# Small row loads ahead of the first weight, and masks, a turned row and two norms behind the third and fourth tile's products

## The chip, the cores and the metric

The kernel runs on one core of a Trainium2 chip. The metric is the device time of one execution in microseconds. A core has TensorE (PE in the profile, its weight loads PEld), VectorE (DVE), ScalarE (ACT), GpSimd (POOL) and SyncE (SP), which here only issues DMAs. Each engine works through its own instructions in order; semaphores tie them together.

## What is computed

One layer of a bidirectional hybrid encoder over 1024 tokens of width 1024, in float32: a norm, one input projection, gated linear attention in both directions beside a pooling mixer, a gated merge with an output projection, then a norm and a SwiGLU feed-forward layer, and a final norm. Only the first two lines of the layer matter for the change:

```python
h = rmsnorm(x, norm_mix[l])
proj = h @ w_in[l]
q, k, v, r, lr_f, lr_b, u, g_a, g_b = jnp.split(proj, split_points, axis=-1)
log_a_f = jax.nn.log_sigmoid((lr_f @ w_decay_up_fwd[l] + b_decay_fwd[l])) / GATE_NORMALIZER
```

The other vectors (`norm_ffn`, `gla_norm`, `pool_scale` and the two decay biases) and the causal masks are used only later in the layer.

## The kernel before

Tokens come in eight tiles of 128. Every float32 operand of a product is split into a high and a low part, and a product is three matmuls: high by high, high by low, low by high (line 275).

The opening computes the value columns of the first two heads, tile by tile. A tile `x` is loaded by `load_x`; its norm is a Square with a sum on ScalarE (line 321, in halves line 463 for the first tiles), an addition on VectorE and a power on GpSimd (lines 306 and 307), and a scaling on VectorE into `xn` (line 311). TensorE turns `xn` by 128x128 pieces into a bank `tr` of PSUM (line 328), and `gain_and_split` reads the bank twice: ScalarE writes the high part `hh` (line 336), VectorE the low part `hl` (line 340), both with the gain that stands in `cols`. The pairs of features `hh`, `hl` are the stationary operands; the moving ones are the eight pieces of a weight, loaded into `vraw` (line 388) and split into `wv` (lines 201 and 202, the difference on VectorE or GpSimd).

`pair_products` multiplies: first tiles 0 and 1 together, with the splitting of the weights and the norms of tiles 2 and 3 in between (`first_steps`), then tile 2, between whose first steps the features of tiles 2 and 3 are turned (`next_steps`), then tile 3. What comes out is split again into `vh` on ScalarE and `vl` on VectorE (lines 515 and 517). `low_rank` follows with `lw`, a split small weight (`lraw`), at line 561, and then the projections of the heads.

The order of the work around these products is set by hand. After every product `pump` advances a clock by one (by the width of the product over 512), and a generator that stands in `side` issues its next step when its delay has run down: `begin(norms(4), 1)` asks for the norm of tile 4 one product later, and `norms` then asks for two more until the norm of tile 5.

Small vectors are loaded as rows (line 374), `rows[0]` for the first gain and `rows[1]` for five others; `columns` turns such rows on TensorE (bank `vps`, line 454) and copies them into `cols` on VectorE (line 455). `masks` writes the masks `keep` and `carry` on VectorE (lines 131 to 133); both are used only in the attention.

All loads named here are issued on SP. A DMA bears one of eight semaphores in turn (DMAHW0 to DMAHW7), and a DMA waits until the earlier one that bears its semaphore has landed.

Of the kernel before, what the change touches and what calls it, by code (L numbers as in the profile page):

```python
# [54 lines left out]
def kernel(  # L55
# [38 lines left out]
    def name(s):  # L94
        count[0] += 1
        return f"{s}_{count[0]}"

    def slot(dtype=F32, shape=(2, HALF), s="slot"):
        return slots.tile([P, *shape], dtype, tag="slot", name=name(s))
# [10 lines left out]
    def bank(pool, s="ps"):  # L110
        return pool.tile([P, HALF], F32, tag=pool.name, name=name(s))

    def as_f32(ap):
        return ap.bitcast(F32)
# [14 lines left out]
    def masks():  # L129
        for n in range(4):  # L130
            nc.vector.tensor_copy(keep[:, n, :], keepf[:, :P])
        nc.vector.memset(carry[:, :, :], 1.0)
        nc.vector.memset(carry[:, :, 0:1], 0.0)
# [56 lines left out]
    def begin(gen, delay=0.0):  # L190
        side.append([gen, delay])

    def finish_side():
        while side:
            for _ in side[0][0]:
                pass
            side.pop(0)
# [49 lines left out]
    def fetch():  # L247
        src = next(order, None)
        if src is not None:
            loaded.append(load(*src))  # L250

    def prepare():
        if not loaded:
            fetch()
        if loaded:
            ready.append(Weights(loaded.pop(0)))

            credit[0] = -2.0
# [18 lines left out]
    def mm3(ps, a, b, first, last, onto=False):  # L277
        products(ps, a, b, first, last, onto)
        pump(ps.shape[-1] / HALF)
# [15 lines left out]
    def tokens(pair, t):  # L295
        return tuple(p[:, (t % 4) * P : (t % 4 + 1) * P] for p in pair)
# [53 lines left out]
    def to_features(xn, t0, act, gain):  # L350

        for kp in range(KT // 2):
            ps = bank(ps_g, "tr")
            for i in range(2):
                transpose_tile(ps, xn[i], i, kp)
            gain_and_split(ps, kp, t0, act, gain)
            yield 1
# [5 lines left out]
    rows = [tmp.tile([n, P], F32, tag="t2", name="rows") for n in (8, 32)]  # L363
# [9 lines left out]
    def load_rows(dst, at, v, n):  # L373
        nc.sync.dma_start(dst[at : at + n, :], v[0].rearrange("(j p) -> j p", p=P))
# [7 lines left out]
    def load_pair_weights(n):  # L382
        for _ in range(n):
            k = len(pair_raw)
            if k % 2 == 0:
                vraw.append(slot(s="vraw"))
            raw = vraw[-1][:, k % 2, :]
            nc.sync.dma_start(raw, w_in[k * P : (k + 1) * P, V0 : V0 + 2 * DV])
            pair_raw.append(raw)
# [7 lines left out]
    def load_other_rows(*which):  # L397
        for i in which:
            load_rows(rows[1], sum(n for _, n in vec_rows[1:i]), *vec_rows[i])
# [1 line left out]
    load_x(0, 2)  # L401
    load_x(1)
    load_rows(rows[0], 0, *vec_rows[0])
    load_other_rows(1, 2)
    load_pair_weights(6)
    load_x(2)
    load_pair_weights(1)
    load_x(3)
    load_pair_weights(1)
    nc.sync.dma_start(lraw[:, :, :], w_in[:, LR0:U0].rearrange("(k p) c -> p k c", p=P))  # L410
    load_other_rows(3, 4, 5)
    nc.gpsimd.memset(uraw[:, :, :, :], 0.0)

    hT = Activations("h")
# [1 line left out]
    def norm_x(t):  # L416
        rs = norm_scale(xt[t % 4][:, :], xn[t % 4], "n1")
        scale_by(xn[t % 4][:, :], xt[t % 4][:, :], rs)
        if t + 4 < NT:
            load_x(t + 4)  # L420

    def norms(t0):
        for t in (t0, t0 + 1):
            norm_x(t)
            yield 2
# [26 lines left out]
    def columns(src, at, n):  # L452
        vps = bank(ps_g, "vps")
        nc.tensor.transpose(vps[:, :n], src[:, :], ident[:n, :n])
        nc.vector.tensor_copy(cols[:, at : at + n], vps[:, :n])
# [45 lines left out]
    def pair_products(ts, before=None):  # L501
        banks = [bank(ps_mm) for _ in ts]
        for k in range(KT):
            if before:
                before(k)
            for ps, t in zip(banks, ts):
                mm3(ps[:, :], tokens(hT(k, t // 4), t), pair_w[k], k == 0, k == KT - 1)
        for ps, t in zip(banks, ts):
            for h in range(2):
                if t // 4 == len(pair_v[h]):  # L510
                    pair_v[h].append((slot(F32R, (4, DV), "vh"), slot(F32R, (4, DV), "vl")))
            parts = [[part[:, t % 4, :] for part in v[t // 4]] for v in pair_v]
            halves = [ps[:, h * DV : (h + 1) * DV] for h in range(2)]
            for (hi, _), src in zip(parts, halves):
                nc.scalar.copy(hi, src)
            for (hi, lo), src in zip(parts, halves):
                nc.vector.tensor_tensor(lo, src, as_f32(hi), op=ALU.subtract)
# [19 lines left out]

    next_features = to_features(xn[2:], 2, hT, g_mix)
    pair_products((0, 1), first_steps)
    masks()  # L540
    columns(rows[1], 8, 32)
    fetch()
    begin(norms(4), 1)
    for d, w_up in enumerate((w_decay_up_fwd, w_decay_up_bwd)):
        for i in range(4):
            load_up(i, d, w_up)
    pair_products((2,), next_steps)
    finish_side()
    begin(norms(6), 0.5)
    begin(to_features(xn, 4, hT, g_mix), 1)  # L550
    begin(to_features(xn[2:], 6, hT, g_mix), 2)
    low_rank_weights()
    prepare()
    pair_products((3,))
    lrT = slot(F32R, (2, HALF), "lrT")

    def low_rank(half):
# [1467 lines left out]
```

## Time and profile before

| | us |
|---|---|
| median of three runs | 1384.52 (1384.5 to 1385.35) |
| profiled execution | 1383.06 |
| its span | 1381.0 |
| TensorE busy | 1367.8 |
| VectorE, ScalarE, GpSimd busy | 835.4, 641.7, 748.6 |
| TensorE's waits for hl (line 340), two of them | 1.3 |

The mean granted clock of TensorE is 0.999 of full speed. Times in the rows of the trace are from the span's start. A row of the timeline has its start, its duration, engine, line, operation, what is written and read, and in brackets the idle time of that engine just before it with what ended it. Matmuls are pipelined, so that rows of TensorE overlap, and the distance of two starts tells its pace better than the durations.

### The profile page before, as it was taken

The page shows a single profiled execution, that of the slowest core. Times are in us where ns is not written, and L with a number is a line of the kernel's source. Part 1 is how long each engine was busy: PE and PEld are TensorE (multiplying, and loading weights), DVE is VectorE, ACT ScalarE, POOL GpSimd, SP SyncE. Part 2 cuts the span into 40 slices and gives each one's busy share as a digit, 9 for nine tenths or more (in the row PEclk, how much of TensorE's full clock was granted, in tenths as well). Part 3 has the DMA queues.
Part 4 walks back from the last instruction along what each step waited for, and adds up shares of the span by engine and source line. Part 5 has one row for each costly group of instructions (what it writes and reads, how often), then busy time and mean ns, then how long its engine had stood idle before and what let it go on. Part 6 is the DMA issues. An engine that isn't in the chain of part 4 may idle for free. (4 is left out here: it accounts for less than half of the span.)

```text
span 1381.0 us, 18211 instructions
## 1 busy us (share of the span) xinstructions
PE 1367.8 (99%) x6514; PEld 1145.9 (83%) x6514; DVE 835.4 (60%) x1025; ACT 641.7 (46%) x1170; POOL 748.6 (54%) x554
## 2 busy tenths in 40 slices
PE   8999999999999999999999999999999999999998
PEld 7888899988888888888888888888888888888886
DVE  5364656567845886687884855555655556343374
ACT  6465756654334544554346633333333334444352
POOL 3222616132288546668665276666666667455453
PEclk9999999999999999999999999999999999999999
DMA  7111414322478668996517355555444447985561
GB/s 226 31 55 53 138 50 134 107 63 77 137 210 292 200 217 265 358 406 227 189 61 244 115 175 175 176 175 175 160 141 140 146 139 264 386 305 186 169 213 76
DMA packets 166730, 243.60 MB, mean 176 GB/s; under 512 B 10952, under 2 KB 95984, under 8 KB 166640
## 3 DMA queue, kind: packets, MB, share of 16 engines
q1 hardware_dynamic: 166496, 242.18, 52.1%
q8 instruction: 51, 0.84, 0.2%
q14 instruction: 39, 0.32, 0.1%
q10 hardware_dynamic: 144, 0.26, 0.0%
HBM read 164.55 MB, written 77.86 MB: 176 GB/s over the span
## 5 line engine op out<-in xcount | busy, mean ns | idle before, releaser
L202 POOL TENSOR_TENSOR wl<-fs,wh 128x512 fp32r<-128x512 f32 x120 | 167.4, 1399 | 160.2 <-ACT wh L201 103.3
L275 PE MATMUL ps<-gh,wh 128*128 128x512 f32 x616 | 240.5, 390 | 0.0
L275 PE MATMUL ps<-gl,wh 128*128 128x512 f32 x616 | 239.8, 389 | 0.3 <-DVE gl L1594 0.3
L275 PE MATMUL ps<-gh,wl 128*128 128x512 f32 x616 | 239.7, 389 | 0.0
L202 POOL TENSOR_TENSOR wl<-fraw,wh 128x512 fp32r<-128x512 f32 x90 | 129.5, 1439 | 63.6 <-ACT wh L201 61.2
L275 PE MATMUL ps<-hh,wh 128*128 128x512 f32 x376 | 151.7, 403 | 0.0
L202 POOL TENSOR_TENSOR ol<-gor,oh 128x1024 fp32r<-128x1024 f32 (+1 forms) x42 | 101.6, 2423 | 85.7 <-ACT oh L201 71.3
L275 PE MATMUL ps<-hh,wl 128*128 128x512 f32 x376 | 146.7, 390 | 0.0
L275 PE MATMUL ps<-hl,wh 128*128 128x512 f32 x376 | 146.5, 390 | 0.0
L275 PEld LDWEIGHTS ps<-gl,wh 128*128 128x128 f32 x616 | 115.6, 188 | 24.6 <-DVE gl L1594 0.7
L275 PEld LDWEIGHTS ps<-gh,wh 128*128 128x128 f32 x616 | 115.7, 188 | 24.0 <-ACT hb L1613 0.2
L275 PEld LDWEIGHTS ps<-gh,wl 128*128 128x128 f32 x616 | 115.6, 188 | 23.9
L202 POOL TENSOR_TENSOR wl<-raw,wh 128x512 fp32r<-128x512 f32 x40 | 55.0, 1385 | 120.9 <-ACT wh L201 111.1
L275 PE MATMUL ps<-oh,oh 128*128 128x512 f32 x308 | 119.8, 389 | 0.0
L275 PE MATMUL ps<-ol,oh 128*128 128x512 f32 x308 | 119.8, 389 | 0.0
L275 PE MATMUL ps<-oh,ol 128*128 128x512 f32 x308 | 119.8, 389 | 0.0
L202 POOL TENSOR_TENSOR wl<-wraw,wh 128x512 fp32r<-128x512 f32 x56 | 92.3, 1678 | 42.6 <-ACT wh L201 42.5
L202 DVE TENSOR_TENSOR ol<-wor,oh 128x1024 fp32r<-128x1024 f32 (+1 forms) x42 | 63.0, 1511 | 68.2 <-ACT oh L201 55.7
L201 ACT CAST wh<-fs 128x512 fp32r<-128x512 f32 x120 | 73.7, 614 | 27.8 <-DVE fs L1013 26.5
L275 PEld LDWEIGHTS ps<-hh,wl 128*128 128x128 f32 x376 | 70.6, 188 | 15.0
L275 PEld LDWEIGHTS ps<-hl,wh 128*128 128x128 f32 x376 | 70.8, 188 | 13.0
L275 PEld LDWEIGHTS ps<-hh,wh 128*128 128x128 f32 x376 | 70.7, 188 | 12.9
(269 smaller groups left out, 3116.9 us busy)
## 6 DMA issues: line engine op xcount, KB each, us to landing
fraw<-in_w_ffn_in_dram SPq DMA_DIRECT2D x44, 512.0 KB, 6.6
gor<-g_out SPq DMA_DIRECT2D x35, 512.0 KB, 7.4
g_out<-s SPq DMA_DIRECT2D x44, 256.0 KB, 2.0
raw<-in_w_in_dram SPq DMA_DIRECT2D x40, 256.0 KB, 4.2
fraw<-in_w_in_dram SPq DMA_DIRECT2D x20, 512.0 KB, 6.7
wor<-t_out SPq DMA_DIRECT2D x20, 512.0 KB, 5.4
g_out<-g SPq DMA_DIRECT2D x33, 256.0 KB, 2.6
x<-in_x_dram SPq DMA_DIRECT2D x15, 512.0 KB, 3.7
```

The lines of the kernel that those rows point to most:

```text
L201: nc.scalar.copy(hi, src)
L202: eng.tensor_tensor(lo, src, as_f32(hi), op=ALU.subtract)
L275: nc.tensor.matmul(ps, a[i], b[j], start=first and n == 0, stop=last and n == 2, skip_group_check=onto)
```

## The change

The loads of the third to fifth of the other rows move ahead of the weights on SP. `masks` moves from behind the products of tiles 0 and 1 to behind those of tile 3, and the turning of `rows[1]` to behind those of tile 2. The norms of tiles 4 and 5 get a delay of 3.5 in place of 1.

```diff
     load_rows(rows[0], 0, *vec_rows[0])
-    load_other_rows(1, 2)
+    load_other_rows(1, 2, 3, 4, 5)
     load_pair_weights(6)
...
     nc.sync.dma_start(lraw[:, :, :], w_in[:, LR0:U0].rearrange("(k p) c -> p k c", p=P))
-    load_other_rows(3, 4, 5)
...
     pair_products((0, 1), first_steps)
-    masks()
-    columns(rows[1], 8, 32)
     fetch()
-    begin(norms(4), 1)
+    begin(norms(4), 3.5)
...
     pair_products((2,), next_steps)
     finish_side()
+    columns(rows[1], 8, 32)
...
     pair_products((3,))
+    masks()
```

On SP, at the start of the program, the loads from the gain of the attention's norm to the tile 2 of `x` (`x_122`) stood so before, with the semaphores for which each waits:

```order
L374 DMA rows<-in_gla_norm_dram 8x128
L388 DMA vraw_138<-in_w_in_dram 128x512 x2
L388 DMA vraw_141<-in_w_in_dram 128x512 [waits DMAHW0_49]
L388 DMA vraw_141<-in_w_in_dram 128x512 [waits DMAHW1_49]
L388 DMA vraw_144<-in_w_in_dram 128x512 [waits DMAHW2_49]
L388 DMA vraw_144<-in_w_in_dram 128x512 [waits DMAHW3_49]
L371 DMA x_122<-in_x_dram 128x1024 [waits DMAHW4_49]
```

The same place now:

```order
L374 DMA rows<-in_gla_norm_dram 8x128
L374 DMA rows<-in_pool_scale_dram 8x128
L374 DMA rows<-in_b_decay_fwd_dram 4x128
L374 DMA rows<-in_b_decay_bwd_dram 4x128 [waits DMAHW0_49]
L388 DMA vraw_141<-in_w_in_dram 128x512 [waits DMAHW1_49]
L388 DMA vraw_141<-in_w_in_dram 128x512 [waits DMAHW2_49]
L388 DMA vraw_144<-in_w_in_dram 128x512 [waits DMAHW3_49]
```

DMAHW2 is borne by the load of the second tile, the third DMA of the program. Four weights were issued before the wait for it, and now there is one.

On VectorE, behind the products of tiles 0 and 1 (`ps_229` is the sum of tile 1, `tr_386`, `tr_404` and `tr_416` are the turned pieces of tiles 2 and 3, `x_120` is tile 4), the rows were:

```order
L517 TENSOR_TENSOR vl_355<-ps_229,vh_354 128x256
L131 CAST keep<-keepf 128x128 x4
L132 MEMSET carry 128x512
L133 MEMSET carry 128x8
L455 COPY cols<-vps_370 128x32
L340 SCALAR_TENSOR_TENSOR hl_261<-tr_386,cols,hh_260 128x256 x2
L306 TENSOR_SCALAR n1rs_400<-n1ms_398 128x1
L311 TENSOR_SCALAR xn_124<-x_120,n1rs_400 128x1024
L340 SCALAR_TENSOR_TENSOR hl_285<-tr_404,cols,hh_284 128x256 x2
L340 SCALAR_TENSOR_TENSOR hl_316<-tr_416,cols,hh_315 128x256 x2
```

There they are now (the turned pieces are called `tr_377`, `tr_389` and `tr_401`):

```order
L516 TENSOR_TENSOR vl_355<-ps_229,vh_354 128x256
L340 SCALAR_TENSOR_TENSOR hl_261<-tr_377,cols,hh_260 128x256 x2
L340 SCALAR_TENSOR_TENSOR hl_285<-tr_389,cols,hh_284 128x256 x2
L340 SCALAR_TENSOR_TENSOR hl_316<-tr_401,cols,hh_315 128x256 x2
L306 TENSOR_SCALAR n1rs_418<-n1ms_416 128x1
L311 TENSOR_SCALAR xn_124<-x_120,n1rs_418 128x1024
```

The masks and the copy have left this place, and the three pairs of `hl` stand ahead of the norm of tile 4.

Behind the products of tile 3 (`ps_453`), the masks stand on VectorE now between `vl` and the features of the tiles from 4 on:

```order
L516 TENSOR_TENSOR vl_355<-ps_453,vh_354 128x256
L131 CAST keep<-keepf 128x128 x4
L132 MEMSET carry 128x512
L133 MEMSET carry 128x8
L340 SCALAR_TENSOR_TENSOR hl_580<-tr_574,cols,hh_579 128x256 x2
```

Before, the last row followed the first one here directly.

## The prediction, made before the changed kernel ran

> **What bounds the kernel now.** I read the page's totals first, then the waits of TensorE over the whole span, to see whether anything but TensorE's own work sets the end.
>
> ```profile
> span 1381.0 us, 18211 instructions
> PE 1367.8 (99%) x6514; PEld 1145.9 (83%) x6514; DVE 835.4 (60%) x1025; ACT 641.7 (46%) x1170; POOL 748.6 (54%) x554
> PE ps L275 <- DVE hl L340: 1.3, 2, 0.7
> PE tr L328 <- DVE xn L311: 1.2, 1, 1.2
> PE op L275 <- DVE p L202: 0.4, 2, 0.2
> ```
>
> TensorE is busy for 99% of the span, and each wait row (total us, times, longest) is small. Of these three the first two lie ahead of 30 us; every other later wait is at most as long as the third. The busy time by stretch (TensorE first) says the same of the middle: 1 us idle in 500, and 0.7 in 700.
>
> ```profile
> 100.00:600.00 500.00, 498.99 (x2618) 428.33 (x2618) 318.31 (x443) 261.91 (x535) 245.14 (x188) 1.00 0.52 170
> 600.00:1300.00 700.00, 699.31 (x3112) 577.78 (x3111) 420.78 (x424) 292.46 (x458) 439.76 (x282) 1.00 0.57 195
> ```
>
> So a microsecond won or lost early reaches the end: later no wait is long enough to swallow it. The change acts before 50 us, and I look for what TensorE waits for there. The timeline of the third tile's products (start, duration, engine, idle before):
>
> ```profile
> 25.60 0.71 PE L275 MATMUL ps<-wv,hh 128*128 128x512 f32 x2
> 26.99 0.50 PE L275 MATMUL ps<-wv,hl 128*128 128x512 f32 x1 [0.68 <-DVE hl L340]
> 27.33 0.63 PE L275 MATMUL ps<-wv,hh 128*128 128x512 f32 x2
> 29.25 0.50 PE L275 MATMUL ps<-wv,hl 128*128 128x512 f32 x1 [0.61 <-DVE hl L340]
> 29.58 0.62 PE L275 MATMUL ps<-wv,hh 128*128 128x512 f32 x2
> 32.32 0.62 PE L275 MATMUL ps<-wv,hh 128*128 128x512 f32 x2
> 33.00 0.62 PE L275 MATMUL ps<-wv,hh 128*128 128x512 f32 x2
> ```
>
> One step of the contraction (two hh, one hl product) takes 33.00 - 32.32 = 0.68 us undisturbed. From 25.60 to 29.58 three steps should take 2.04 and take 3.98: the two waits, 1.29 us as idle rows, cost 1.94 us of cadence.
>
> **What the change takes away.** Both waits are for hl, which VectorE writes late. Its rows, with what ScalarE and GpSimd do beside:
>
> ```profile
> 23.82 1.41 DVE L517 TENSOR_TENSOR vl<-ps,vh 128x256 fp32r<-128x256 f32 x4
> 23.93 0.89 ACT L336 ACTIVATE hh<-tr,cols 128x256 fp32r<-128x256 f32 x2
> 24.66 1.12 ACT L321 ACTIVATE xn<-x 128x1024 f32<-128x1024 f32 x1
> 25.15 0.62 DVE L131 CAST keep<-keepf 128x128 uint8<-128x128 f32 x4
> 25.82 0.48 DVE L132 MEMSET carry<- 128x512 bf16 x1
> 26.46 0.87 DVE L340 SCALAR_TENSOR_TENSOR hl<-tr,cols,hh 128x256 fp32r<-128x256 f32 x2
> 27.46 0.55 POOL L307 TENSOR_TENSOR n1rs<-n1rs,half_neg 128x1 f32<-128x1 f32 x1 [7.20 <-DVE n1rs L306]
> 28.05 0.75 DVE L311 TENSOR_SCALAR xn<-x,n1rs 128x1024 f32<-128x1024 f32 x1 [0.66 <-POOL n1rs L307]
> 28.72 1.65 DVE L340 SCALAR_TENSOR_TENSOR hl<-tr,cols,hh 128x256 fp32r<-128x256 f32 x4
> 31.09 0.75 DVE L311 TENSOR_SCALAR xn<-x,n1rs 128x1024 f32<-128x1024 f32 x1 [0.66 <-POOL n1rs L307]
> 35.73 0.60 PE L328 MATMUL tr<-ident,xn 128*128 128x128 f32 x4
> ```
>
> First wait: the masks and the copy of the turned row hold VectorE from 25.15 to 26.46, while hh is ready at 24.82. Second: the norm of tile 4 makes VectorE idle 0.66 for GpSimd and then scale for 0.75, ahead of the hl. In the changed order the three hl pairs follow the vl directly: with 0.87 each they run at about 25.2 to 26.0, 26.0 to 26.9 and 26.9 to 27.8. Without waits TensorE wants the first hl at 26.06 (25.60 plus two products), when its first half has been written for 0.4 us; the second pair's first half is ready near 26.5 against 27.4 wanted, the third's near 27.4 against 28.8. ScalarE's Square also goes behind the hh, so these come earlier, not later. I take the whole 1.94, and 1.29 as the least.
>
> What is late next? The two delayed norms: their chain (Square 1.1, GpSimd 0.55, scaling 0.75) then ends near 31.2, where it ends now at 31.84 (31.09 + 0.75), and TensorE turns that tile at 35.73, 1.94 earlier after the change: 2.6 us of room. The turned row is 0.24 of TensorE in either place, and its column copy precedes nothing that waits: nothing.
>
> **The masks' new place.** They stand behind the fourth tile's vl:
>
> ```profile
> 41.96 0.74 DVE L517 TENSOR_TENSOR vl<-ps,vh 128x256 fp32r<-128x256 f32 x2
> 42.62 0.86 DVE L340 SCALAR_TENSOR_TENSOR hl<-tr,cols,hh 128x256 fp32r<-128x256 f32 x2
> 44.04 0.88 DVE L340 SCALAR_TENSOR_TENSOR hl<-tr,cols,hh 128x256 fp32r<-128x256 f32 x2 [0.56 <-ACT hh L336]
> ```
>
> About 1.2 us of masks (0.62 + 0.48 and a small one) delay these hl, of which 0.56 goes into VectorE's idle time. The cover is that the products then running use the first four tiles' features, and that five banks take the turned tiles. I charge 0; without the cover 1.2.
>
> **The opening, the uncertain term.** Three more row loads now pass SP ahead of the weights, and at most eight DMAs are outstanding by the semaphores in the order. So what waits for the second tile's landing (SP's wait of 2.0 us below) is no longer the fifth weight, but the second. The first weight goes out about 1 us later, by three row issues of some 0.3; ScalarE, which casts it ahead of the first hh, has 1.74 us of idle time there: hidden.
>
> ```profile
> 2.92 0.29 SPq L374 DMA_DIRECT2D rows<-in_gla_norm_dram  x1
> SPq L388 <- DMA x<-in_x_dram: 2.0, 1, 2.0
> 7.07 0.63 ACT L463 ACTIVATE xn<-x 128x512 f32<-128x512 f32 x1 [2.28 <-DMA x<-in_x_dram]
> 10.11 0.47 ACT L336 ACTIVATE hh<-tr,cols 128x256 fp32r<-128x256 f32 x1 [1.74 <-PE tr L328]
> 10.49 0.61 ACT L201 CAST wv<-vraw 128x512 fp32r<-128x512 f32 x1
> 17.51 0.63 ACT L201 CAST wv<-vraw 128x512 fp32r<-128x512 f32 x1
> 20.30 0.75 DVE L311 TENSOR_SCALAR xn<-x,n1rs 128x1024 f32<-128x1024 f32 x1 [0.85 <-POOL n1rs L307]
> 21.52 0.60 PE L328 MATMUL tr<-ident,xn 128*128 128x128 f32 x4
> vraw<-in_w_in_dram SPq DMA_DIRECT2D x1, 256.0 KB, 6.9
> x<-in_x_dram SPq DMA_DIRECT2D x2, 256.0 KB, 2.6
> GB/s 0 0 0 0 0 0 0 147 197 262 352 369 377 410 246 197 229 295 295 338 289 270 357 320 393 393 418 393 393 418 401 303 238 205 205 320 344 336 361 352
> DMA packets 2227, 3.21 MB, mean 321 GB/s; under 512 B 1182, under 2 KB 1198, under 8 KB 2227
> ```
>
> The 40 slices of the GB/s row are 0.25 us each from 0, the last row is the mean from 8 to 18 us; the 6.9 us to landing is the last weight's, issued at 9.33, so landed at 16.2.
>
> A gain: the second tile lands at 7.07, and the opening chain (its sum, the scalings, the turns, the first product) starts there. Summing the slices, 1.05 MB, the first two tiles, had moved by 5.45, and 1.64 MB by 7.0: weights moved beside the tile. With all but one weight out of its way it lands between 6.05 (5.45 plus 0.6, as the first half tile: moved by 2.8, landed at 0.80 + 2.6 = 3.4) and 7.07. I take the middle, 6.55: 0.5 us gained, bounds 0 and 1.02.
>
> A loss: the second weight goes out only then, so the DMA engines run dry. Now the fifth weight is issued at 7.07, and its bytes show about 1.6 us later, in the slices behind the 205s. From the second weight to the eighth with two tiles between there are 2.88 MB, 9.0 us at 321 GB/s. So the last weight lands at 6.55 + 1.6 + 9.0 + 0.6 and a little for a full queue, about 18.0. Wanted: from its cast at 17.51 to the fourth tile's scaling (20.30 + 0.75) are 3.54 us, and TensorE turns that tile at 21.52; so a landing after 17.98, less the 0.5 won, delays TensorE. That is 0.5 lost. The second weight lands near 6.55 + 2.6 = 9.2 to 10 and is cast at 10.49 now, about 10.0 then: in time. Gain and loss cancel: 0, with bounds of -1.0 and, if the second weight goes out at 7.07 and takes 4.75 us (the middle of 2.6 and 6.9), +1.3, its lateness against 10.49.
>
> Here a rule weighs in. The Trainium skill, DMA: Bandwidth & Descriptors, Queues, rings and completion order, says that an SDMA engine consumes the descriptors of a ring in order. By it weights issued behind the tile take nothing from it; the sum would be -1.4 instead of -1.9. The trace speaks half against it, by the 1.64 MB moved at a landing of a tile that stands within the first 1.05.
>
> **Sum.** -1.94 + 0 + 0 = -1.9 us. The profiled execution took 1383.06 (span 1381.0 and 2.06 around it), so 1381.1 by its own time; the runs' median, 1384.52, lies 1.46 above it, and the same step from there gives 1382.6.
>
> **The rivals.** (1) The tile lands no earlier, at 7.07, and the weights still lose 0.5: -1.94 + 0.5 = -1.4, 1383.1. For it: the ring's order; against it: the slices. (2) The tile lands at 6.05 and the stream keeps up: -1.94 - 1.02 = -2.96, 1381.6. For it: 400 GB/s slices; against it: the dry spell. (3) Masks in the new place delay TensorE by their 1.2: -0.7, 1383.8, if the half-filled VectorE there has less room than its idle row shows. (4) Slower: the load stream, restarted late, runs at the 205 GB/s of its weakest slices. 2.88 MB then take 14.0 us, the last weight lands at 7.07 + 1.6 + 14.0 + 0.6 = 23.3, 5.3 us late, and +3.4 is left: 1387.9. It turns the sign from a landing past 19.9 on; the mean of 321 speaks against it. That nothing changes is hardly possible: VectorE's order does change.
>
> **The numbers.** Forecast 0.46, rival 1 0.20, rival 2 0.22, rival 3 0.05, rival 4 0.07. 0.2% is 2.8 us, about what a measurement of this kernel can tell from no change; only rival 2 passes it downward and only rival 4 upward. So faster 0.22, same 0.71, slower 0.07. The range runs from just under rival 2, 1381.3, to the forecast with the least gain (1.29) and the most loss (1.3), 1384.5, rounded up.
>
> **Right or wrong.** The profile after should have no row of TensorE waiting for hl in the third tile's products, the two norms' Squares behind the hh, and the masks behind the fourth tile's vl with no new wait of TensorE. The second tile's landing, the second weight's cast and the fourth tile's turn give the opening: first hh 0.5 earlier, near 9.6, and the first turn of the third and fourth tiles near 21.5. I am wrong if TensorE waits for a wv or xn for over a microsecond before 22 us, or if a wait after 50 us takes the gain back.

## The result, and the profile after

The changed kernel takes 1380.62 us in the median (1380.12 to 1382.23, fourteen runs), and the kernel before, run in turn with it, 1383.77 (1382.81 to 1385.65, fourteen runs). The ratio is 0.9978, with a 95% interval from 0.9969 to 0.9986: a gain of 3.15 us, and of 1.9 to 4.3 by the interval. The forecast was 1382.6, its range began at 1381.3, and the result lies below it.

The profiled execution of the changed kernel took 1382.23 us, the most of its fourteen. Its totals, and the five longest waits of TensorE (total us, times, longest):

```profile
span 1380.2 us, 18211 instructions
PE 1368.3 (99%) x6514; PEld 1146.9 (83%) x6514; DVE 836.3 (61%) x1025; ACT 641.7 (46%) x1170; POOL 748.0 (54%) x554
PE warm L473 <- POOL ident masks.py:199: 1.4, 1, 1.4
PE vps L453 <- DMA rows<-in_norm_mix_dram: 1.2, 1, 1.2
PE sc L858 <- DVE st L842: 0.5, 2, 0.2
PE op L275 <- DVE p L202: 0.4, 2, 0.2
PE tr L328 <- DVE xn L311: 0.4, 1, 0.4
```

The row of 1.3 us for hl is gone. The middle is as idle as it was, 1.1 us in 500 and 0.7 in 700 (busy time by stretch, TensorE first), so no later wait took the gain back:

```profile
100.00:600.00 500.00, 498.89 (x2617) 428.05 (x2617) 318.26 (x442) 260.98 (x533) 243.89 (x187) 1.00 0.52 170
600.00:1300.00 700.00, 699.35 (x3112) 577.92 (x3111) 421.41 (x425) 292.45 (x459) 439.69 (x282) 1.00 0.57 195
```

The third tile's products in the timeline of the changed kernel, with the features, the norm and the turned row beside them:

```profile
24.42 0.19 PEld L275 LDWEIGHTS ps<-wv,hl 128*128 128x128 f32 x1 [0.28 <-DVE hl L340]
24.68 1.41 DVE L516 TENSOR_TENSOR vl<-ps,vh 128x256 fp32r<-128x256 f32 x4
24.78 2.58 ACT L336 ACTIVATE hh<-tr,cols 128x256 fp32r<-128x256 f32 x6
26.00 2.44 DVE L340 SCALAR_TENSOR_TENSOR hl<-tr,cols,hh 128x256 fp32r<-128x256 f32 x6
26.24 0.71 PE L275 MATMUL ps<-wv,hh 128*128 128x512 f32 x2
27.02 0.62 PE L275 MATMUL ps<-wv,hh 128*128 128x512 f32 x2
27.71 0.62 PE L275 MATMUL ps<-wv,hh 128*128 128x512 f32 x2
28.39 0.62 PE L275 MATMUL ps<-wv,hh 128*128 128x512 f32 x2
29.25 0.75 DVE L311 TENSOR_SCALAR xn<-x,n1rs 128x1024 f32<-128x1024 f32 x1 [0.66 <-POOL n1rs L307]
30.52 0.24 PE L453 MATMUL vps<-ident,rows 32*128 32x32 f32 x1
```

The six hl follow each other in one row of 2.44 us, and three steps take 28.39 - 26.24 = 2.15 us where they took 3.98: 1.83 won. A smaller wait ahead of them is new: with the turned row gone from its old place, TensorE comes sooner to the product of an earlier hl, and loading that hl as weights waits 0.28 (the row at 24.42). The masks stand behind the fourth tile's vl; the first low-rank product and one of the turns beside them:

```profile
37.51 0.48 PE L560 MATMUL ps<-hh,lw 128*128 128x512 f32 x1
40.74 0.74 DVE L516 TENSOR_TENSOR vl<-ps,vh 128x256 fp32r<-128x256 f32 x2
41.40 0.62 DVE L131 CAST keep<-keepf 128x128 uint8<-128x128 f32 x4
42.07 0.48 DVE L132 MEMSET carry<- 128x512 bf16 x1
42.84 0.60 PE L328 MATMUL tr<-ident,xn 128*128 128x128 f32 x4
```

No row of TensorE waiting for the hl behind the masks appears.

The opening was slower, not faster. First the kernel before, with the first low-rank product (line 561 there, 560 above) and the turn that answers to the one above, then the changed one:

```profile
8.55 1.09 PE L328 MATMUL tr<-ident,xn 128*128 128x128 f32 x8 [1.21 <-DVE xn L311]
10.64 0.74 PE L275 MATMUL ps<-wv,hh 128*128 128x512 f32 x2 [0.35 <-ACT hh L336]
38.34 0.47 PE L561 MATMUL ps<-hh,lw 128*128 128x512 f32 x1
43.66 0.60 PE L328 MATMUL tr<-ident,xn 128*128 128x128 f32 x4
```

```profile
6.61 0.63 ACT L462 ACTIVATE xn<-x 128x512 f32<-128x512 f32 x1 [1.73 <-DMA x<-in_x_dram]
6.62 0.22 PE L453 MATMUL vps<-ident,rows 8*128 8x8 f32 x1 [1.25 <-DMA rows<-in_norm_mix_dram]
8.09 1.97 PE L328 MATMUL tr<-ident,xn 128*128 128x128 f32 x8 [0.43 <-DVE xn L311]
11.47 0.73 PE L275 MATMUL ps<-wv,hh 128*128 128x512 f32 x2
18.36 0.63 ACT L201 CAST wv<-vraw 128x512 fp32r<-128x512 f32 x1
22.38 0.60 PE L328 MATMUL tr<-ident,xn 128*128 128x128 f32 x4
```

The second tile landed at 6.61, 0.46 earlier than before, and yet the first product starts 0.83 later: it comes 4.86 us behind the landing, and came 3.57 behind it. The eight turns take 1.97 us in place of 1.09. The stretches of the changed kernel say why (the number ahead of the last two is the granted clock):

```profile
8.00:8.50 0.50, 0.41 (x2) 0.41 (x3) 0.43 (x2) 0.36 (x1) 0.47 (x1) 0.56 0.75 279
8.50:11.00 2.50, 2.50 (x14) 2.43 (x12) 1.08 (x2) 0.05 (x1) 0.00 (x0) 0.50 0.99 350
11.00:12.00 1.00, 0.86 (x4) 0.30 (x3) 0.52 (x2) 0.95 (x3) 0.00 (x0) 0.76 1.12 395
```

TensorE ran at half its clock for 3.4 us, by the record of the granted clock from 8.06 to 11.47. So in this execution the opening lost 0.83 and the third tile won, from its first turn to the first low-rank product, 16.82 - 15.13 = 1.69 (38.34 - 21.52 before, 37.51 - 22.38 now); the rest is level in sum, and the spans differ by 0.8. The median gain of 3.15 is another matter, and the experiments went after it.

### The profile page after: what moved, and what is told of

Its sections match the earlier page's. It is cut to its first block, busy times and chain, and to the rows that moved or that the text cites. A ratio compares the mean times of both kernels' runs of the same rounds, so it can differ in the third digit from the quotient of the medians.

```text
span 1380.2 us, 18211 instructions
## 1 busy us (share of the span) xinstructions
PE 1368.3 (99%) x6514; PEld 1146.9 (83%) x6514; DVE 836.3 (61%) x1025; ACT 641.7 (46%) x1170; POOL 748.0 (54%) x554
```

## The experiments

The theory is the prediction's: the third tile's two waits, and an opening that gives and takes. Its rivals: the row loads carry much of the gain, or the clock's drop is tied to one of the two orders, so that the median gains more than one profile shows. The times below are medians with the number of runs, beside the kernel before in the same session.

**One part alone.** The row loads moved, and nothing else:

```diff
-    load_other_rows(1, 2)
+    load_other_rows(1, 2, 3, 4, 5)
...
-    load_other_rows(3, 4, 5)
```

> Only the three row loads are moved ahead of the weights. Theory A (the gain is in the third tile's products): both waits for hl stay, 0.7 and 0.6 us; the second tile lands near 6.6 instead of 7.07, and the time falls by about 0.5 us if TensorE's clock stays up in the opening, and rises by about 0.8 if the clock is halved there as in the profile of the changed kernel. Theory B (the loads carry the larger part of the 3.15): 1.3 us or more faster.

Measured: 1382.43 (11) beside 1383.74 (29), 0.9991 [0.9982, 1.0]. The third tile's two waits are still there in its waits of TensorE:

```profile
PE ps L275 <- DVE hl L340: 1.3, 2, 0.7
```

Everything but the row loads:

```diff
-    masks()
-    columns(rows[1], 8, 32)
-    begin(norms(4), 1)
+    begin(norms(4), 3.5)
     pair_products((2,), next_steps)
     finish_side()
+    columns(rows[1], 8, 32)
     pair_products((3,))
+    masks()
```

> Only the masks, the turned row and the norms are moved; the row loads stay behind the weights. Theory A: no wait for hl in the third tile's products, 1.7 us less from that tile's first turn to the fourth tile's last, second tile landing at 7.07 as before, time 1.7 to 1.9 us lower. Theory B: 1.9 lower at most, and the rest of the 3.15 missing.

Measured: 1379.99 (7) beside 1383.74, 0.9973 [0.9963, 0.9984]. The new order alone gives the whole gain; with the row loads moved as well the median is nominally 0.63 higher.

The masks and the turned row without the norms' delay (the diff above without the `begin` lines):

> Only the masks and the turned row are moved, the norms keep the delay of 1. Theory A, two separate waits: the first wait for hl goes (1.05 us of cadence), the second (0.88) stays, since the norm of tile 4 still stands between the first and the second pair of hl: about 1.0 us faster. Rival: one queue that is late as a whole, so that the norm is absorbed once the masks are gone: 1.7 faster, like both.

Measured: 1381.7 (11), 0.9986 [0.9977, 0.9994]; and the norms' delay alone (only the `begin` lines):

> Only the norms get the delay of 3.5, masks and turned row stay. Theory A, two separate waits: the first wait for hl stays, the second goes: about 0.9 us faster. Rival: one queue that is late as a whole: the second wait is only pushed on and less than 0.5 is gained.

Measured: 1382.14 (11), 0.9988 [0.998, 0.9997]. In each one of the two waits is left, the second in the masks' kernel and the first in the norms':

```profile
PE ps L275 <- DVE hl L340: 0.5, 1, 0.5
```

```profile
PE ps L275 <- DVE hl L340: 0.7, 1, 0.7
```

From the third tile's first turn to the first low-rank product both take 15.92 us: 0.90 won by each, 1.69 by both. The two waits are separate and add up to within 0.11.

The medians don't add up so well: 1.3 for the row loads, 2.0 for the masks and the turned row and 1.6 for the norms are 4.95 in sum, where all together win 3.15. Each interval still holds what the profile shows (for the norms 0.4 to 2.8, and 0.90), so the surplus is scatter or something that no profile shows.

**The clock.** To see whether the half clock falls to one of the two orders, the warm-up of TensorE ahead of the first turns was made longer in three kernels: in the kernel before, in the kernel without the row loads, and in the changed one.

```diff
-WARM = 20
+WARM = 28
```

> The kernel before with 28 instead of 20 warming turns ahead of the first row's turn, so that TensorE has no idle stretch of half a microsecond before 7 us. Theory H1 (ordinary executions of the kernel before lose TensorE's clock in the opening in some of the runs, 1.3 us each time): 0.5 to 1.3 us faster in the median, the upper half of the spread (1384 to 1385.4) gone. Theory H2 (the opening plays no part in the spread): no change within 0.3 us, or slower if the longer warming delays the first row's turn.

> The same warming with the masks, the turned row and the norms moved, the row loads not. H1: 1.7 us (1.69 measured between the first turn of the third tile and the first low-rank product) below the kernel before with 28 turns. H2: 3.75 below it, as without the warming.

> The same warming with the whole change. If the row loads bring the second tile in earlier on average, as predicted (0.5 us): 0.3 to 0.5 below the order-only kernel with 28 turns. If the landing only varies by execution: equal to it within 0.3. Full granted clock from 6 to 12 us in the profile.

Measured: 1383.72 (11), 1380.3 (8) and 1381.26 (11), beside 1384.09 (24): 0.9999 [0.999, 1.0008], 0.9974 [0.9964, 0.9984] and 0.9979 [0.997, 0.9988]. The longer warm-up leaves each about where it was, and the order is still worth 3.4 beside it (1383.72 and 1380.3). It has a price of its own: in these three profiles the first product comes 3.77 to 4.02 behind the second tile's landing, in place of 3.57. The kernel before was also profiled again as it is:

> The kernel before once more, for a second profile of the same code. If the second tile's landing is set by the order of the loads: 7.07 again within 0.1 us. If it varies by execution: anywhere from 6.2 to 7.1, and 14.45 us from there to the third tile's first turn unless the clock falls.

Measured: 1383.85, span 1381.8. In this execution the kernel before ran at half pace in the opening itself:

```profile
6.17 0.63 ACT L463 ACTIVATE xn<-x 128x512 f32<-128x512 f32 x1 [1.21 <-DMA x<-in_x_dram]
7.94 1.92 PE L328 MATMUL tr<-ident,xn 128*128 128x128 f32 x8
11.13 0.73 PE L275 MATMUL ps<-wv,hh 128*128 128x512 f32 x2 [0.35 <-ACT hh L336]
```

The tile landed 0.9 earlier than in the first profile, and the first product started 0.5 later. This is not a fall of the clock, but a late rise. In every profile the turns of the warm-up start 0.21 us apart at first, and 0.11 apart from the moment on at which the record of the granted clock begins; the views count the time ahead of it as 1.00. That moment lies between 4.31 and 7.39 us in sixteen of the eighteen profiles, but at 10.28 in this one and at 10.86 in that of `best_rows` below. In the first profile of the changed kernel the clock had risen at 4.65, fell at 8.06 and rose again at 11.47. So both the landing and the clock change from one execution to the next, whatever the kernel.

Late rise or fall, it costs the first product 1.3 us or more in three of the twelve profiles with the short warm-up and in none of the six with the longer one. These are too few to call it rarer there. The executions without a profile don't tell either. Their one figure is the granted clock averaged over the execution, and it has no part of a late rise. It does have a part of another fall, which every profile shows between 1374 and 1380 us, when the last products are done. So the mean is 0.998 in the profiles of `w_fill` and `best_order`, whose openings lost nothing, and 0.999 in the two with the late rise. Executions of the kernel before with a mean of 0.998 or lower have a median of 1384.6 (30 of 93) and the others 1383.3; in the changed kernel it is 1380.95 (6 of 14) and 1380.57, and in `w_after` the other way round, 1380.5 (3 of 11) and 1381.5. What part the clock has in the median gain is open.

Do the third tile's waits themselves lower the clock in part of the executions, so that taking them away wins more than 1.7? Two ways to ask: fill them with work of TensorE, or double them. On top of the longer warm-up, six turns of the identity in steps 2 and 4 of `next_steps`:

```diff
+        if k in (2, 4):
+            for i in range(6):
+                nc.tensor.transpose(fill[:, i % 4 * P : (i % 4 + 1) * P], ident[:, :], ident[:, :])
...
+    fill = bank(ps_g, "fill")
```

> The kernel before with 28 warming turns, and six idle turns of the identity on TensorE ahead of the third and fifth steps of the third tile's products, where it waits for hl: the same work else. Theory H3 (in ordinary executions the two waits make TensorE's clock fall, which no profile caught): 0.6 us or more below the kernel before with 28 turns (1383.72). Theory H4 (the rest of the difference is scatter of the opening and of the stretches after 120 us): within 0.3 us of it.

and `masks()` written twice, so that its work is done twice:

```diff
+    masks()
     masks()
```

> The kernel before with 28 warming turns, and the masks written twice at the old place. H3 and H4 both: the first wait for hl grows from 0.7 to about 1.9 us, 1.2 more from the third tile's first turn to the first low-rank product (16.82 to 18.0). H3 alone: products behind the waits at half pace for 3.4 us, and so over 19 us for that stretch.

with the same kernel as `w_before` profiled beside them once more:

> The kernel before with 28 warming turns, for a second profile. H3: now and then the third tile's stretch takes 18 us or more instead of 16.8. H4: 16.8 again, and a difference of up to 0.5 us in some stretch after 120 us.

Measured: filled 1382.52 (11) beside 1383.32 (15), 0.9992 [0.9983, 1.0001], which is neither level nor clearly faster; twice the masks 1383.23, span 1381.5; `w_before` again 1383.16, span 1381.1. The wait in the kernel with doubled masks nearly doubled:

```profile
PE ps L275 <- DVE hl L340: 2.5, 2, 1.9
```

It cost 18.10 - 16.82 = 1.28 us from the third tile's first turn to the first low-rank product, the price of the masks, and the clock did not fall, during the waits or behind them (stretches of `w_twice`):

```profile
26.00:30.00 4.00, 1.76 (x7) 1.15 (x7) 3.23 (x12) 1.76 (x4) 0.55 (x1) 1.00 0.41 106
30.00:33.50 3.50, 3.50 (x16) 2.85 (x17) 2.12 (x6) 0.96 (x4) 0.55 (x1) 1.00 0.24 71
```

The seven profiles with both waits left as they were (before three times, `w_before` twice, `e1_rows`, `shift`) took 16.81 to 16.84 there. That the waits lower the clock is not borne out.

**A step later on.** Every kernel with masks or row loads moved, and the one with the masks doubled, gains a further 0.33 us near 129 us, the same in each of its profiles; the kernel before (three profiles), `w_before` (two), the filled kernel and the norms' delay alone don't. There VectorE's `st` row starts 0.37 later in the kernel before than in the changed one (idle 1.82 and 1.45), first before, then the changed kernel:

```profile
128.32 0.48 DVE L843 SCALAR_TENSOR_TENSOR st<-kv,fac,so 128x256 f32<-128x256 f32 x1 [1.82 <-ACT k L740]
```

```profile
127.12 0.48 DVE L842 SCALAR_TENSOR_TENSOR st<-kv,fac,so 128x256 f32<-128x256 f32 x1 [1.45 <-ACT op L926]
```

None of the moved work is near. What the kernels that have the step share is an edit of what VectorE runs ahead of it (with the row loads moved, only of the semaphores it waits for). So six small writes that nothing needs were put ahead of the warm-up of the kernel before, beside a third profile of it:

```diff
+    for _ in range(6):
+        nc.vector.memset(carry[:, :, 0:1], 0.0)
     keep_warm(WARM)
```

> The kernel before with six one-column writes of a mask added to VectorE's stream at the very start, where VectorE is idle until 4.8 us; nothing else moves. Theory H5 (where VectorE's stream stands decides two small delays near 129 and 239 us, whatever the added instructions do): both waits for hl stay (16.82 for the third tile's stretch), but 0.3 us are gained at 129 and 0.3 at 239: 0.4 to 0.7 us faster. Rival (the two delays belong to the moved work itself): no step there, same time within 0.2.

> The kernel before, for a third profile. Landing of the second tile between 6.2 and 7.1; 3.57 us from there to the first product with the clock up, 4.9 with half the clock; 16.82 for the third tile's stretch by H4, 18 or more by H3.

Measured: with the six writes 1382.42 (11) beside 1383.2 (25), 0.9995 [0.9986, 1.0004]; before again 1383.44, span 1381.4. The profile of `shift` has the short idle time:

```profile
127.66 0.48 DVE L845 SCALAR_TENSOR_TENSOR st<-kv,fac,so 128x256 f32<-128x256 f32 x1 [1.45 <-ACT op L929]
```

So six more instructions on VectorE, which nothing waits for, take 0.33 us off: an edit of VectorE's stream that has no bearing on `st` is enough, and that is shown. The lateness is not gone in `shift`, but stands two `st` earlier, where TensorE loses nothing by it:

```profile
123.49 0.48 DVE L845 SCALAR_TENSOR_TENSOR st<-kv,fac,so 128x256 f32<-128x256 f32 x1 [1.80 <-ACT op L929]
```

Counted in the traces, with the waits for semaphores, the late `st` is VectorE's 192nd record in all nine profiles that have one: those of the kernel before, of `w_before`, of the filled kernel and of the norms' delay, where TensorE loses 0.33, and those of `shift` and of the doubled masks, where it doesn't. In the other nine the moved masks or row loads have put the count off by one, the 192nd record is a wait or a copy, and no `st` is late. The norms' delay leaves the count as it was. So the place in VectorE's stream decides; what happens at that place, a fetch of instructions perhaps, is not shown. The second step, expected near 239 us, did not come as forecast: `shift` gains 0.19 there, and the changed kernel 0.02 or less in both profiles.

**A version that might beat both.** The order without the row loads, and with the first tile's scaling ahead of the second tile's sum:

```diff
+    for j in range(2):
+        scale_half(0, j)
...
-    for j in range(2):
-        scale_half(0, j)
```

> Masks, turned row and norms moved, row loads not, and the first tile's scaling put ahead of the second tile's sum on VectorE. With the clock up the chain from the second tile's landing still goes over GpSimd: first product 0 to 0.2 us earlier. But TensorE turns the first tile about a microsecond sooner and idles less, so that fewer executions lose the clock and each loses less: 0.1 to 0.6 below the order-only kernel's 1379.99 (3.8 to 4.3 below the kernel before).

and the same two lines in the changed kernel, with a second profile of the changed kernel beside it:

> The same with the row loads moved too. If the loads' place matters on average (0.5 us by the earlier landing): below the kernel without it by 0.3 to 0.5. If the landing only varies by execution: equal within 0.3, or up to 0.4 above it, by the 0.36 us that the order-only kernels spend less around the span.

> The changed kernel, for a second profile: third tile's stretch 15.13 again, steps of -0.3 at 129 and 239 us against the kernel before again. Second tile's landing between 6.2 and 7.1, and 3.57 us to the first product if the clock stays up, 4.9 if not.

Measured: 1380.11 (9) and 1380.99 (11) beside 1383.2 (25): 0.9978 [0.9968, 0.9988] and 0.9985 [0.9976, 0.9994]; the changed kernel again 1381.07, span 1379.0. In `best_order` the first product comes 3.24 behind the landing in place of 3.57, but 1380.11 is no better than the 1379.99 without this edit, and `best_rows` was at half pace in its profile (5.07). It is 0.88 above `best_order`, more than either case expected. No version is clear of the changed kernel by the intervals. The second profile of the changed kernel shows what its first one hid, an early landing at full clock:

```profile
6.16 0.63 ACT L462 ACTIVATE xn<-x 128x512 f32<-128x512 f32 x1 [1.26 <-DMA x<-in_x_dram]
17.82 0.62 ACT L201 CAST wv<-vraw 128x512 fp32r<-128x512 f32 x1 [0.42 <-DMA vraw<-in_w_in_dram]
20.36 0.75 DVE L311 TENSOR_SCALAR xn<-x,n1rs 128x1024 f32<-128x1024 f32 x1 [0.68 <-POOL n1rs L307]
20.61 0.38 PE L328 MATMUL tr<-ident,xn 128*128 128x128 f32 x2
21.17 0.44 PE L328 MATMUL tr<-ident,xn 128*128 128x128 f32 x2 [0.18 <-DVE xn L311]
```

The last weight is waited for, the fourth tile's scaling ends at 21.11, and TensorE waits for it within its turns: from the third tile's first turn, 20.61, to the first low-rank product it takes 15.57 in place of 15.13.

The profiles side by side, each column a time or a distance in us:

| kernel | second tile lands | to the first product | third tile's first turn to low rank | low rank to the last matmul | span |
|---|---|---|---|---|---|
| before | 7.07 | 3.57 | 16.82 | 1335.35 | 1381.0 |
| before again | 6.17 | 4.96 | 16.83 | 1335.61 | 1381.8 |
| before, third | 6.86 | 3.57 | 16.82 | 1335.91 | 1381.4 |
| changed | 6.61 | 4.86 | 15.13 | 1335.37 | 1380.2 |
| changed again | 6.16 | 3.57 | 15.57 | 1335.55 | 1379.0 |
| `e1_rows` | 6.19 | 3.57 | 16.82 | 1334.93 | 1379.7 |
| `e2_order` | 6.39 | 3.57 | 15.13 | 1334.91 | 1378.2 |
| `e3_masks` | 6.58 | 3.57 | 15.92 | 1335.58 | 1379.8 |
| `e4_norms` | 6.37 | 3.57 | 15.92 | 1336.18 | 1380.2 |
| `w_twice` | 6.46 | 3.57 | 18.10 | 1335.19 | 1381.5 |
| `shift` | 6.73 | 3.57 | 16.84 | 1335.35 | 1380.7 |

Apart from the late weight of the second profile of the changed kernel, the way from the third tile's first turn to the low-rank product is the same to 0.07 wherever the order is the same (`w_order` and `best_order`, which are not in the table, have 15.20 and 15.19). The landing scatters by 0.9 between executions of one kernel, and the way to the last matmul by 0.6, as much as some edits move them; over all profiles that way goes from 1334.58 (`w_after`) to 1336.93 (`best_rows`).

## Why the prediction was wrong

The mechanism held. What failed is the sum: the base that it was counted from stood 0.75 us too high, and terms that it had at nothing were not nothing.

**The two waits: right, and a little mis-sized.** The 1.94 measured 1.69. Three steps take 2.15 and not 2.04, since the first of them stands behind a turn and takes 0.78 (26.24 to 27.02), which leaves 1.83. The move of the turned row costs 0.14, where the prediction had it at nothing: it takes about a third of a microsecond of TensorE in either place, not 0.24, and its going laid open the small wait at 24.42. The norms' delay has the room it was given: no wait of TensorE follows from it in `e4_norms`.

**The masks' new place: right.** They were charged 0. Ahead of them the changed kernel is 0.83 earlier than before by the first low-rank product, and 0.82 earlier at a turn just behind them (42.84 and 43.66). The third rival, masks that delay TensorE by 1.2, is out.

**The opening: the mechanism is there, the base was wrong.** The step took one execution's landing, 7.07, for what the kernel does. Thirteen profiles with the loads as before have it from 6.17 to 7.07, 6.63 in the mean; five with the rows moved from 6.16 to 6.61, 6.36 in the mean. So the predicted 6.55 lies within that range, and the gain is 0.28 by the means, not 0.5, with ranges that overlap. The third tile's first turn, forecast near 21.5, came at 22.38 and at 20.61. The late last weight is as predicted in the second profile of the changed kernel (0.44 against 0.5) and absent in the first, where TensorE was late itself and the DMA engines moved 359 GB/s on average between 8 and 18 us in place of 321. Of the other three profiles with the rows moved, only that of `e1_rows` has a wait for this weight (0.29), and it costs TensorE nothing. The sum of 0 stands about. The rivals, a tile that lands no earlier and one that lands at 6.05 with a stream that keeps up, can't be told apart by such a scatter; the fourth, a stream at 205 GB/s, is out. The same goes for the rule of the Trainium skill, DMA: Bandwidth & Descriptors, Queues, rings and completion order, weighed in the prediction: a difference of 0.28 between overlapping ranges neither bears it out nor speaks against it.

**Missing from the sum: the clock.** Half the clock behind the landing costs 1.3 to 1.4 us up to the first product (4.86 and 4.96 in place of 3.57), and 1.8 in `best_rows` (5.07 in place of the 3.24 of `best_order`). It struck one of three profiles of before and one of two of the changed kernel. The Trainium skill, TensorE: Matmul & The Clock Gate, Part 1: The HAM clock gate, says that TensorE falls to half speed after an idle window of about 3.4 us, and that this window runs free of the kernel. The length and the free run agree with the traces: the fall lasts from 8.06 to 11.47, and from the first rise to the last fall it is 1368.74 or 1372.16 us in every profile, 401 or 402 times 3.413, wherever the first rise lies. The idle window does not, since TensorE's idle rows ahead of the fall are 1.25 and 0.43 us. It moves single executions, and whether it moves the medians of the two orders apart, no run could show.

**Missing from the sum: 0.33 us at VectorE's `st`.** It is in every profile of the changed kernel. The trace of before shows one `st` that waits longer than its neighbours (1.82 and 1.45), but not that the change would take this away. Nor is it seen to reach the end: from the first low-rank product to the last matmul the changed kernel takes 1335.46 in the mean of its two profiles, and the kernel before 1335.62 in the mean of three that scatter by 0.6.

**The base.** The forecast stood on the median of three runs, 1384.52; fourteen give 1383.77. Of the 2.0 us between forecast and result 0.75 are this alone. From 1383.77 the same steps lead to 1381.8 and the range begins at 1380.55, just below the result. So the step that put the result outside the range was to count from the median of three runs, 1.46 above the profiled execution. The three runs lay within 0.85 us of each other, and the fourteen span 2.8.

**What adds up and what stays open.** By the profiles the change wins 1.69 in the third tile, 0.33 at `st` if that reaches the end, and 0.28 in the mean landing: 2.3 us, inside the measured 1.9 to 4.3. The remaining 0.85 of the median gain has no place in the profiles, and the clock in the opening is a rival that no run settles. The kernel without the row loads is nominally 0.6 to 1.0 us faster than the one with them in three comparisons, the first across two sessions (1379.99 and 1380.62, 1380.3 and 1381.26, 1380.11 and 1380.99), though alone these loads seem to win 1.3 (0 to 2.5 by the interval). Some 0.35 of it is time around the span (below), and the rest is not separated by the intervals. Both stay open.

## What to carry to other kernels

Look first for small work on a vector engine that stands ahead of what TensorE wants next and isn't needed for long: here its two waits, 1.3 us of idle rows, were worth 1.7 us of pace, and the masks cost nothing in their new place, where VectorE had idle time. The time of one load in one profile is a draw, not a property of the kernel: take a term like the landing from several profiles, and take the base from more than three runs when the expected gain is a thousandth. Count idle rows as a lower bound, and measure the pace of a full step for the rest.

## What the runs showed of the hardware

- The same load, in the same place of the queue, landed between 6.17 and 7.07 us in thirteen executions of kernels that issue it alike.
- TensorE starts at half pace: the warm-up's turns of 128x128 begin near 1.4 us, 0.21 apart, and come 0.11 apart from 4.31 to 7.39 us on in sixteen profiles, and from 10.28 and 10.86 on in two. The granted clock in the views reads 1.00 meanwhile, so the pace of a known group of instructions tells more.
- The rises and falls of its clock lie on a grid: from the first rise to the last fall it is 401 or 402 times 3.413 us in all eighteen profiles.
- Its clock fell to 0.50 behind 3.41 us in which it had been idle for 1.65 (4.65 to 8.06 in the changed kernel), and stayed at 1.00 behind a stretch of the same grid with 1.68 idle (26.56 to 29.97 in `w_twice`). So the idle time alone does not decide.
- VectorE's 192nd record comes 0.37 us late whenever it is an `st`, in nine profiles of nine, and six added writes in the first microseconds are enough to move that place to another `st`, which brings TensorE's products 0.33 forward.
- The time around the span is 2.00 to 2.15 us in before, the changed kernel and six others, and 1.67 to 1.79 in `e2_order`, `e3_masks`, `w_order`, `w_twice`, `shift` and `best_order`, in every execution of a kernel alike; what sets it was not found.
